# Weighted sums of gathered expert rows: one token's slots per gather and a matmul in place of one slot per gather and a vector add

## The chip, the cores and the metric

The kernel runs on one core of one Trainium2 chip. The metric is the device time of one execution in microseconds (us), lower is better. The core's five engines run side by side, each with its own in-order queue: PE (TensorE, matmuls; PEld is its weight load), DVE (VectorE), ACT (ScalarE), POOL (GpSimd) and SP (SyncE, which here only starts DMAs).

## The reference, cut to what matters

One decoder layer runs for 512 prompt tokens and 32 sample tokens (8 sequences of 4): RMSNorm, an input projection, RWKV-7 time mixing beside windowed attention, an output projection, and then the PEER expert retrieval, which is where the change sits. Each token has 8 heads of 16 chosen experts, so 128 slots; each slot names one of 16,384 rows of `expert_u` and of `expert_v` (1,024 f32 numbers, 4 KB a row).

```python
idx  = ...                                  # (token, 128) expert numbers
gate = softmax(top)                         # (token, 128)
pre  = einsum('td,tkd->tk', hb, eu[idx])    # a dot product per slot
act  = gelu(pre) * gate
out  = einsum('tk,tkd->td', act, ev[idx])   # a scaled sum of 128 rows per token
x    = x + out
y    = rmsnorm(x, final_norm_g)
```

## The kernel before, in words

The prompt is cut into four tiles of 128 tokens. Tiles 1 and 2 (256 tokens) take the expert layer densely: all 16,384 experts in 128 blocks, on PE. Tiles 0 and 3 and the 32 samples gather only the rows that they need. `experts` (L1024) does that: an indirect DMA per step, issued by POOL (L1032), brings 128 rows, one into each partition; 128 steps for `expert_u` (DVE multiplies the buffer by the token's `h2` and sums, `dot`, L1041), then Gelu, then 128 steps for `expert_v` (DVE adds the scaled buffer to `acc`, `add`, L1050). In step k partition p holds the row for slot k of token p. The samples use the 128 partitions as 4 head pairs of 32 tokens, so they take 32 + 32 steps, and at the end `sample_experts` (L1066) brings the four parts together with three small DMAs and four DVE additions. Gathered rows lie in one rotation of five buffers, `gat`; the use of a buffer is written two steps behind its gather (`LAG`, L33).

The program has three stretches. The front (to about 1107 us) holds the projections, the time mixing, attention and the choice of experts (`two_heads`, L970: top-16 searches on DVE). Then `gates` (L1380) spreads the gate values of tiles 1 and 2 into dense tables. Then the dense stage runs its 128 blocks, with tile 3's own front work (`late`, L1507) in its first blocks, and tile 3's gathers beside it.

The gather steps are Python generators in the list `side`; `beside` (L245) takes steps from it. A scheduler then orders the instructions of each engine at build time: what was written earlier has priority, what was written later fills the gaps. `first_gathers` (L1319) puts tile 0's 256 steps into `side`, `sample_heads` appends the samples' 64. No step is written during the front. 280 are written in one go after it (`AHEAD`, L36 and L1552), the other 40 a few at a time between the groups of `gates` (`RATE_G`, L1402) and the first dense blocks (`RATE_D`, L1585); each step's DVE instructions are tied behind a given earlier DVE instruction.

PSUM has eight banks of 128 x 512 f32. In the front six belong to pool `pp` (L1281) as three pairs, `pB` (time mixing), `pC` (attention and the rest) and `pD` (projections), and two to pool `pe` (L232): `pA` (`rwkv_prep`, L282) and `pQ` (`mix_and_retrieve`, L905), one bank each. `fr.close()` (L1361) gives them all back. The dense pool `dp` (L1407) takes all eight: four banks `w`, four `acc`.

Of the kernel before, what the change touches and what calls it, by code (L numbers as in the profile page):

```python
# [32 lines left out]
LAG = 2  # L33
WST = 3
UV = 5
AHEAD = 280  # L36
RATE_G = 0.8
RATE_D = 3.0
LATE = 2
# [74 lines left out]
def hymba_step(ctx, tc, x_prompt, x_sample, cache_k, cache_v, state_wkv, state_shift, meta, norm1_g, w_in, mu, w0,  # L114
# [40 lines left out]
    def gat(shape=(128, D)):  # L155
        return _t(p0, "gat", GAT, shape)

    def px2():
        return _t(p0, "x2", 1, [128, D])
# [19 lines left out]
    def transpose(out, in_):  # L179
# [3 lines left out]
        else:  # L183
            T.matmul(out, in_, ident[:k, :k], start=True, stop=True)


    few = p0.tile([128, 4], F32, name="few")
    epsn, epsg, half3, one = (few[:, i:i + 1] for i in range(4))
# [40 lines left out]
        DM.dma_start(t, const[:, _OFF[c][0]:_OFF[c][0] + 16])  # L229

    er = fr.enter_context(tc.tile_pool(name="er", bufs=1, side="right"))
    pe = fr.enter_context(tc.tile_pool(name="pe", bufs=1, space=PSUM, side="right"))  # L232

    def st(tag, bufs, shape, dt=F32):
        return _t(er if tag in _EARLY else sb, tag, bufs, shape, dt)
# [15 lines left out]
                side.pop(0)  # L251
        due[0] = min(due[0], 1.0)

    def pA():
        return _t(pe, "pA", 1, [128, 512])

    def pB():
        return _t(pp, "pB", 2, [128, 512])

    def pC():  # L260
        return _t(pp, "pC", 2, [128, 512])

    def pD():
        return _t(pp, "pD", 2, [128, 512])

    def pQ():
        return _t(pe, "pQ", 1, [128, 512])

    def h_transposed(h, rows, put, ps):
        for half in range(2):  # L270
# [11 lines left out]
    def rwkv_prep(c0, n, more=None):  # L282
        special, meta_ = n == 40, n == 16
        e = n + 1
        room = [dx([128, D]) for _ in range(3)] if meta_ else None
        pP = pQ if meta_ else pA
        m = (st("mm", 1, [128, 14, 16]) if meta_ else st("m14", 1, [128, 14, 128]))[:, :, 0:n]
        for k0, k1 in ((12, 14), (0, 12)) if more else ((0, 14),):
            DM.dma_start(m[:, k0:k1], mscr[k0:k1, :, c0:c0 + n].rearrange("k p c -> p k c"))
# [10 lines left out]
            gT = m[:, 13, :]  # L300
            A.activation(gT, gT, AF.Sigmoid)
        pw = pP().rearrange("p (a b) -> p a b", a=4)
        pz = (more or pP)().rearrange("p (a b) -> p a b", a=4)
        for b in range(4):
            T.matmul(pw[:, b, 0:n], lora[0:64, b * 128:(b + 1) * 128], th, start=True, stop=True)
            T.matmul(pz[:, b, 0:n], lora[64:128, b * 128:(b + 1) * 128], m[64:128, 12, :], start=True, stop=True)
# [598 lines left out]
    def mix_and_retrieve(items):  # L905
# [37 lines left out]
        for g in range(4):  # L943
            scs = [st(f"sco{x}", 2 - x, [128, 4, 128])[:it[1]] for x, it in enumerate(items[::-1])][::-1]
            for j in range(4):
                if j % 2 == 0:
                    ps = pQ().rearrange("p (i j n) -> p i j n", i=2, j=2)
                hc = 4 * g + j
                wt = weights(w_query, hc)
                p = pD()  # L950
                for k in range(8):
                    T.matmul(p[:, 0:tot], wt[:, k, :], h2T[:, k, :], start=(k == 0), stop=(k == 7))
                qT = st("qq", 2, [128, 160])[:, 0:tot]
                A.copy(qT, p[:, 0:tot])
                for x, (it, o) in enumerate(zip(items, offs)):
                    T.matmul(ps[:it[1], x, j % 2, :], qT[:, o:o + it[1]], skT[:, hc % 2, :], start=True, stop=True)
                if j % 2:
                    for x, (it, sc) in enumerate(zip(items, scs)):
                        A.copy(sc[:, j - 1:j + 1, :], ps[:it[1], x])
            for it, sc in zip(items, scs):  # L960
                if isinstance(it[5], bass.AP):
                    DM.dma_start(it[5][:, 4 * g:4 * g + 4, :], sc)
                else:
                    two_heads(sc, [x[:, 32 * g:32 * g + 32] for x in it[5]], front_tile)
# [56 lines left out]
        V.tensor_tensor(gate, gate, bc(rd.unsqueeze(2), [128, 2, 16]), OP.mult)  # L1021


    def experts(h2, ei, gate, nk, acc, fresh):  # L1024

        pre = _t(p0, "pre", 1, [128, 128])

        def rows(w, use):
            held = []
            for k in range(nk):  # L1030
                r = gat()
                G.indirect_dma_start(out=r, out_offset=None, in_=w[0],  # L1032
                                     in_offset=bass.IndirectOffsetOnAxis(ap=ei[:, k:k + 1], axis=0))
                held.append((k, r))
                if len(held) > LAG:
                    use(*held.pop(0))
                yield True
            for x in held:
                use(*x)

        def dot(k, u):  # L1041
            V.tensor_tensor_reduce(out=u, in0=u, in1=h2, scale=1.0, scalar=0.0, op0=OP.mult, op1=OP.add,
                                   accum_out=pre[:, k:k + 1])
        yield from rows(eu, dot)
        act = _t(p0, "act", 1, [128, 128])
        A.activation(act[:, 0:nk], pre[:, 0:nk], AF.Gelu)
        V.tensor_tensor(act[:, 0:nk], act[:, 0:nk], gate[:, 0:nk], OP.mult)
        acc = acc()

        def add(k, v):  # L1050
            if k == 0 and fresh:
                V.tensor_scalar(acc, v, act[:, 0:1], None, OP.mult)
            else:
                V.scalar_tensor_tensor(acc, v, act[:, k:k + 1], acc, OP.mult, OP.add)
        yield from rows(ev, add)

    def finish(x2, y, rows, dst, gf, kind="F"):

        rms(x2[:rows], y[:rows], rows, gf, kind)
        DM.dma_start(dst, y[:rows])  # L1060

    def final_g(t):
        G.dma_start(t, fin_g.partition_broadcast(128))
        return t

    def sample_experts():  # L1066

        h2S = ph2()
        for kg in range(4):
            G.dma_start(h2S[32 * kg:32 * kg + 32, :], hscr_s)  # L1070
        box = []

        def mk():
            box.append(px2())
            return box[0]
        yield from experts(h2S, plS[0], plS[1], 32, mk, True)
        xs2 = ph2()
        G.dma_start(xs2[0:32, :], xscr_s)
        for kg in range(4):
            part = box[0]  # L1080
            if kg:
                part = gat()
                G.dma_start(part[0:32, :], box[0][32 * kg:32 * kg + 32, :])
            V.tensor_tensor(xs2[0:32, :], xs2[0:32, :], part[0:32, :], OP.add)
        finish(xs2, gat(), 32, y_s.rearrange("b s d -> (b s) d"), final_g(gat()))

    def tile_experts(i, ei, ga, h2, x2=None):
        def mk():
            if x2 is None:
                box.append(px2())  # L1090
                G.dma_start(box[0], xscr[i])
            return box[0]
        box = [] if x2 is None else [x2]
        yield from experts(h2, ei, ga, 128, mk, False)
        finish(box[0], gat(), 128, y_p[0, 128 * i:128 * i + 128, :], final_g(gat()))


    def load_qk(c0, n):
# [9 lines left out]
                   t[:, j, :].rearrange("p (b f) -> p b f", f=5)[:, :, 0:4])  # L1108
        return qk

    def place(c):
        return _t(p0, "ei" + c, 1, [128, 128], I32), _t(p0, "ga" + c, 1, [128, 128])

    plS, pl0, pl1 = place("s"), place("0"), place("1")
    dsel = [[_t(p0, f"dsel{i}{c}", 1, [128, 128]) for c in range(3)] for i in range(2)]
    ycats, zs = {}, {}

# [199 lines left out]
    gather_mark = []  # L1317

    def first_gathers():  # L1319
        side.append(tile_experts(0, *pl0, *held))  # L1320
        gather_mark.append(len(marks))

    def sample_heads():
# [56 lines left out]
    def gates(its, sel, ps, put):  # L1380
# [6 lines left out]
        for n, t8 in enumerate(range(0, 128, 8)):  # L1387
# [12 lines left out]
                put(t8 + q0, p)  # L1400
            with tc.issue_after(marks[-1]):
                beside(RATE_G)  # L1402


    ND = 256
# [101 lines left out]
    def late():  # L1507
# [28 lines left out]
        for g in range(4):  # L1536
# [10 lines left out]
                    A.copy(sc[:, j0 + j, :], p[:, 128:256])  # L1547
                yield True
            two_heads(sc, [x[:, 32 * g:32 * g + 32] for x in pl1], late_tile)
        side.append(tile_experts(3, *pl1, x2))  # L1550

    for n in range(AHEAD):  # L1552
        with tc.issue_after(marks[gather_mark[0]]):
            beside(1)
    more = late()
    its = one_hot_table()
    sels = [sel_transposed(0, dps, dt_("selT", 1, [128, 3, 128])), sel_transposed(1, dps, dt_("lsc", 1, [128, 3, 128]))]
# [73 lines left out]
```

## Time and profile before

| | us |
|---|---|
| median of 3 runs | 2249.78 (2248.66 to 2256.09) |
| the profiled execution, its own time | 2252.27 |
| its span, first to last instruction | 2250.5 |
| PE / DVE / ACT / POOL busy | 1852.8 / 1721.2 / 864.3 / 1499.9 |
| mean granted TensorE clock | 0.869 |

The span is what the trace shows; the execution's own time has 1.8 us around it. A busy time is the sum over the whole span, so it hides that different engines set the pace in different stretches. The granted clock is a share of 2.4 GHz; at any moment it is 1.0 or 0.5, and a number between is a mean over a stretch.

### The profile page before, as it was taken

The page shows a single profiled execution, that of the slowest core. Times are in us where ns is not written, and L with a number is a line of the kernel's source. Part 1 is how long each engine was busy: PE and PEld are TensorE (multiplying, and loading weights), DVE is VectorE, ACT ScalarE, POOL GpSimd, SP SyncE. Part 2 cuts the span into 40 slices and gives each one's busy share as a digit, 9 for nine tenths or more (in the row PEclk, how much of TensorE's full clock was granted, in tenths as well). Part 3 has the DMA queues.
Part 4 walks back from the last instruction along what each step waited for, and adds up shares of the span by engine and source line. Part 5 has one row for each costly group of instructions (what it writes and reads, how often), then busy time and mean ns, then how long its engine had stood idle before and what let it go on. Part 6 is the DMA issues. An engine that isn't in the chain of part 4 may idle for free.

```text
span 2250.5 us, 37333 instructions
## 1 busy us (share of the span) xinstructions
PE 1852.8 (82%) x13915; PEld 1718.7 (76%) x13915; DVE 1721.2 (76%) x3221; ACT 864.3 (38%) x1803; POOL 1499.9 (67%) x1135
## 2 busy tenths in 40 slices
PE   5899975586759769878256887899999999999995
PEld 5889874474637657867255887899999999999995
DVE  5543446888778878899799579987666788879897
ACT  6644422212223314232277534343444444343333
POOL 0110114878764876457577656899888999999996
PEclk9999996555756668989588999999999999999998
DMA  7532472777785898978476777799889998998886
GB/s 225 153 100 75 131 201 89 254 255 235 257 278 171 267 311 275 304 253 288 142 215 219 265 272 260 265 327 330 330 328 328 331 319 315 313 316 309 307 301 208
DMA packets 310155, 569.51 MB, mean 253 GB/s; under 512 B 32787, under 2 KB 194565, under 8 KB 309830
## 3 DMA queue, kind: packets, MB, share of 16 engines
q0 software_dynamic: 84048, 305.70, 39.6%
q1 hardware_dynamic: 225926, 261.43, 35.8%
q8 instruction: 109, 1.79, 0.3%
q14 instruction: 72, 0.59, 0.1%
HBM read 543.07 MB, written 24.60 MB: 252 GB/s over the span
## 4 chain that ended last, share of the span: by engine, by line
PE 37%; DVE 22%; issue 14%; POOL 13%; DMA 11%; ACT 2%; SPq 0%; DVEq 0%; POOLq 0%; ACTq 0%
POOL gat L1032 7%; DVE gat L126 4%; DVE x L126 4%; PE acc L1477 3%; PE pD L218 3%; PE acc L1478 3%; DVE uL L126 3%; PE acc L1476 3%; PE w L1461 3%; PE w L1458 3%; PE w L1459 3%; DMA gat<-in_expert_u_dram,ei 2%; PE w L1444 2%; DMA gat<-in_expert_v_dram,ei 2%; POOL aL L1469 2%
## 5 line engine op out<-in xcount | busy, mean ns | idle before, releaser
L126 DVE SCALAR_TENSOR_TENSOR x<-gat,act,x 128x1024 f32<-128x1024 f32 x287 | 495.3, 1726 | 34.1 <-DMA gat<-in_expert_v_dram,ei 31.9
L1032 POOL DMA_INDIRECT gat<-in_expert_u_dram,ei x256 | 353.7, 1382 | 114.6 <-DVE pre L126 51.7
L1032 POOL DMA_INDIRECT gat<-in_expert_v_dram,ei x256 | 335.8, 1312 | 127.9 <-issue 32.7
L1451 POOL TENSOR_TENSOR vL<-uv,vH 128x1024 fp32r<-128x1024 f32 x128 | 314.7, 2459 | 14.0 <-ACT vH L1450 12.0
L1477 PE MATMUL acc<-aL,vH 128*128 128x256 f32 x1024 | 295.5, 290 | 21.8 <-POOL aL L1469 21.5
L1476 PE MATMUL acc<-aH,vH 128*128 128x256 f32 x1024 | 295.0, 295 | 3.4 <-ACT aH L1468 3.4
L1478 PE MATMUL acc<-aH,vL 128*128 128x256 f32 x1024 | 291.4, 286 | 0.0
L1458 PE MATMUL w<-dhH,uH 128*128 128x256 f32 x1024 | 254.2, 285 | 3.7 <-ACT lsc L1547 1.7
L1459 PE MATMUL w<-dhL,uH 128*128 128x256 f32 x1024 | 252.9, 284 | 0.0
L126 DVE CUSTOM_DVE_ANT_0 gat<-gat,h 128x1024 f32<-128x1024 f32 x160 | 215.6, 1357 | 48.8 <-DMA gat<-in_expert_u_dram,ei 45.0
L1450 ACT CAST vH<-uv 128x1024 fp32r<-128x1024 f32 x128 | 134.5, 1051 | 228.5 <-issue 105.4
L1477 PEld LDWEIGHTS acc<-aL,vH 128*128 128x128 f32 x1024 | 199.2, 195 | 27.9 <-POOL aL L1469 27.8
L126 DVE CUSTOM_DVE_ANT_0 gat<-gat,lx 128x1024 f32<-128x1024 f32 x128 | 204.7, 1623 | 9.0 <-DMA gat<-in_expert_u_dram,ei 9.0
L1458 PEld LDWEIGHTS w<-dhH,uH 128*128 128x128 f32 x1024 | 197.7, 193 | 4.8 <-ACT lsc L1547 2.1
L1478 PEld LDWEIGHTS acc<-aH,vL 128*128 128x128 f32 x1024 | 199.3, 195 | 0.0
L1476 PEld LDWEIGHTS acc<-aH,vH 128*128 128x128 f32 x1024 | 195.2, 194 | 3.9 <-ACT aH L1468 3.9
L1459 PEld LDWEIGHTS w<-dhL,uH 128*128 128x128 f32 x1024 | 197.7, 193 | 0.1
L126 DVE TENSOR_TENSOR uL<-w,uH 128x512 fp32r<-128x512 f32 x256 | 167.4, 682 | 16.4 <-ACT uH L1446 14.1
L1469 POOL TENSOR_TENSOR aL<-ac,aH 128x256 fp32r<-128x256 f32 x128 | 141.3, 1104 | 33.6 <-ACT aH L1468 31.3
L1461 PE MATMUL w<-dhH,uL 128*128 128x256 f32 x1024 | 153.5, 289 | 11.4 <-DVE uL L126 11.1
L126 DVE TENSOR_TENSOR ac<-w,gl 128x128 f32<-128x128 f32 x128 | 49.7, 389 | 139.2 <-ACT w L1463 116.5
L1446 ACT CAST uH<-w 128x512 fp32r<-128x512 f32 x256 | 139.3, 591 | 27.3 <-PE w L1444 16.8
(575 smaller groups left out, 4264.7 us busy)
## 6 DMA issues: line engine op xcount, KB each, us to landing
uv<-in_expert_u_dram SPq DMA_DIRECT2D x128, 512.0 KB
uv<-in_expert_v_dram SPq DMA_DIRECT2D x128, 512.0 KB
wst<-in_w_query_dram SPq DMA_DIRECT2D x48, 512.0 KB
wst<-in_w_out_dram SPq DMA_DIRECT2D x24, 512.0 KB
wst<-in_w_in_dram SPq DMA_DIRECT2D x20, 512.0 KB
h2T<-in_w_in_dram SPq DMA_DIRECT2D x20, 512.0 KB
gscr<-uv SPq DMA_DIRECT2D x10, 1024.0 KB
gl<-gscr SPq DMA_DIRECT2D x16, 512.0 KB
```

Of the source, the lines that this page charges most:

```text
L126: r = getattr(nc.vector, name)(*args, **kw)
L1032: G.indirect_dma_start(out=r, out_offset=None, in_=w[0], in_offset=bass.IndirectOffsetOnAxis(ap=ei[:, k:k + 1], axis=0))
L1446: A.copy(uH[:, ks, :], p)
L1450: A.copy(vH, vn)
L1451: G.tensor_tensor(vL, vn, vH.bitcast(F32), OP.subtract)
L1458: T.matmul(pre, uH[:, k, :], hH[:, k, :], start=(k == 0), stop=False)
L1459: T.matmul(pre, uH[:, k, :], hL[:, k, :], start=False, stop=False)
L1461: T.matmul(pre, uL[:, k, :], hH[:, k, :], start=False, stop=(k == 7))
L1469: return (vH, vL, aH, aL), G.tensor_tensor(aL, ac, aH.bitcast(F32), OP.subtract).ins
L1476: T.matmul(o, vH[:, ds_], aH, start=(j == 0 and d % 2 == 0), stop=False, skip_group_check=True)
L1477: T.matmul(o, vH[:, ds_], aL, start=False, stop=False, skip_group_check=True)
L1478: T.matmul(o, vL[:, ds_], aH, start=False, stop=(j == 127), skip_group_check=True)
```

## The change

For tile 0 and the samples (not for tile 3) the `expert_v` half of `experts` is done another way. The table of expert numbers is turned by PE (a transpose through PSUM, then a copy to `eO`), so that one gather now fetches the 128 slots of *one token*, a slot per partition. The activations are turned in the same way (`at`). ACT makes a 128 x 32 matrix `z`, zero but for one column, which holds the token's 128 activations; PE multiplies: `z` stationary, the 128 x 1,024 buffer moving in two halves of 512, and adds the result to two PSUM banks (`v0`, `v1`), where the token's row is 32q + t. Gathers are used in pairs, of two different q, with four matmuls a pair. 128 gathers stay 128, and 32 stay 32. Two DVE additions from PSUM end a tile; the samples' three part DMAs and four additions go.

The two banks are a pool `vp`; the six others become one rotation `w` for all that `pA`, `pB`, `pC`, `pD` and `pQ` served. `vp` is closed before `dp` opens, so all 320 steps are written ahead of `gates`, and `AHEAD` is gone. The helper tiles `ef` and `at` take the one buffer of `pre`.

```diff
-AHEAD = 280
+    unit = p0.tile([128, 63], F32, name="unit")
+    V.memset(unit, 0.0)
+    V.memset(unit[:, 31:32], 1.0)
-    pe = fr.enter_context(tc.tile_pool(name="pe", bufs=1, space=PSUM, side="right"))
+    vs = ctx.enter_context(ExitStack())
+    vp = vs.enter_context(tc.tile_pool(name="vp", bufs=1, space=PSUM, side="right"))
-    def pA(): return _t(pe, "pA", 1, [128, 512])
-    def pB(): return _t(pp, "pB", 2, [128, 512])
...
+    def bank():
+        return _t(pp, "w", 6, [128, 512])
+    pB = pC = pD = bank
-        pP = pQ if meta_ else pA
+        pP = more or bank
...
+    def summed(ei, nk, per, out):
+        def add(act):
+            n = 4 * per
+            et = _t(p0, "eO", 1, [128, 128], I32)
+            order = [per * (i % 4) + i // 4 for i in range(n)]
+            def turned(src):
+                p = _t(vp, "v0", 1, [128, 512])
+                if nk == 128:
+                    T.transpose(p[:, 0:128], src, ident)
+                else:
+                    for g in range(4):
+                        gs = slice(32 * g, 32 * g + 32)
+                        T.matmul(p[gs, 0:32], src[gs, 0:32], ident[gs, gs], start=True, stop=True)
+                return p[:, 0:n]
+            ef = _t(p0, "pre", 1, [128, 128])
+            V.tensor_copy(ef[:, 0:nk], ei[:, 0:nk])
+            A.copy(et[:, 0:n].rearrange("p (r q) -> p r q", q=4), turned(ef).rearrange("p (q r) -> p r q", q=4))
+            p = turned(act)
+            at = _t(p0, "pre", 1, [128, 128])
+            A.copy(at[:, 0:n], p)
+            va = [_t(vp, f"v{x}", 1, [128, 512]) for x in range(2)]
+            pair = []
+            def use(k, r):
+                q, t = k % 4, k // 4
+                z = _t(p0, "z", 4, [128, 32])
+                A.mul(z, unit[:, 31 - t:63 - t], at[:, order[k]:order[k] + 1])
+                pair.append((q, t, z, r))
+                if len(pair) == 2:
+                    for x in range(2):
+                        for q, t, z, r in pair:
+                            T.matmul(va[x][32 * q:32 * q + 32, :], z, r[:, 512 * x:512 * x + 512], start=(t == 0),
+                                     stop=(t == per - 1))
+                    pair.clear()
+            yield from rows(ev, et, n, use)
+            out(va)
+        return add
+    def plus(x, va):
+        for h in range(2):
+            V.tensor_tensor(x[:, 512 * h:512 * h + 512], x[:, 512 * h:512 * h + 512], va[h], OP.add)
...
+    while side:
+        with tc.issue_after(marks[gather_mark[0]]):
+            beside(1)
+    vs.close()
     ND = 256
     dn = ctx.enter_context(tc.tile_pool(name="dn", bufs=1))
-    for n in range(AHEAD):
-        with tc.issue_after(marks[gather_mark[0]]):
-            beside(1)
```

## Rows read from the trace of the kernel before

**Rows 1.** Busy us of the five engines by stretch, clock, DMA share, GB/s.
```profile
670.00:900.00 230.00, 189.48 (x1089) 156.09 (x1088) 182.97 (x253) 77.42 (x189) 153.79 (x125) 0.71 0.78 254
900.00:1110.00 210.00, 143.39 (x1094) 129.78 (x1094) 194.19 (x713) 50.55 (x146) 123.21 (x140) 0.86 0.80 257
1110.00:1252.00 142.00, 87.64 (x519) 80.45 (x520) 134.42 (x125) 105.33 (x164) 103.61 (x66) 0.81 0.62 197
1252.00:1400.00 148.00, 128.17 (x979) 123.62 (x979) 108.73 (x310) 59.62 (x129) 86.58 (x79) 0.95 0.80 280
```

**Rows 2.** The same, instructions on `act` alone: busy us of DVE and ACT.
```profile
900.00:1110.00 210.00, 44.95 (x34) 0.00 (x0) 0.86 0.80 257
1110.00:1252.00 142.00, 24.24 (x15) 0.23 (x1) 0.81 0.62 197
1252.00:1400.00 148.00, 28.55 (x19) 0.00 (x0) 0.95 0.80 280
```

**Rows 3.** Chain that ended last, shares by line: 900:1110, 1110:1252 and 1252:1400.
```profile
by line: DVE x L126 13.8%; DVE gat L126 12.0%; DVE idxu L126 8.4%; DMA wst<-in_w_query_dram 7.0%; issue 7.0%; DVE hl L126 6.4%; DVE dsel L126 5.9%; DVE vals L126 5.6%; DVE sel L126 4.9%; DVE ce L126 4.5%; DVE sco L126 3.8%; DMA gat<-in_expe
...
by line: DVE uL L126 33.0%; issue 22.9%; DVE vH L126 8.5%; PE w L1399 8.1%; DVE gat L126 7.6%; DVE x L126 6.8%; POOL vH L1394 4.0%; ACT uH L1392 2.8%; DMA uv<-hscr 2.7%; PE w L1424 2.6%; PE w L1368 0.9%; POOL gat L1032 0.7%; ACT lsc L1369 0
...
by line: DMA xscr<-lx 9.9%; PE w L1521 7.0%; DVE lsm L126 6.4%; issue 5.7%; PE w L1543 4.8%; DMA gat<-x 4.8%; DVE x L126 4.7%; DVE lidx L126 4.6%; DVE gat L126 4.5%; PE w L1461 4.2%; PE w L1458 3.9%; PE w L1459 3.7%; DVE uL L126 3.4%; DVE l
```

**Rows 4.** Instructions on `gat`: ns min/median/max, first and last start (first row 670:1010).
```profile
L126 DVE SCALAR_TENSOR_TENSOR x<-gat,act,x x128: 1243/1283/3686, 675.8 to 1003.4; 128x1024 f32<-128x1024 f32 x128
...
L1032 POOL DMA_INDIRECT gat<-in_expert_v_dram,ei x256: 932/1017/2605, 663.8 to 2230.9; - x128
L1032 POOL DMA_INDIRECT gat<-in_expert_u_dram,eis x32: 937/976/2015, 1026.3 to 1150.9; - x32
L1032 POOL DMA_INDIRECT gat<-in_expert_v_dram,eis x32: 933/1188/1873, 1158.5 to 1331.6; - x32
```

**Rows 5.** Groups by shape, 1110:1252, DVE: busy us, mean ns, idle before.
```profile
L126 DVE CUSTOM_DVE_ANT_0 gat<-gat,h 128x1024 f32<-128x1024 f32 x11 | 18.5, 1688 | 0.0
```

**Rows 6.** The chain that ended last, in order of time: waits for gathered rows.
```profile
784.01 9.26 DMA gat<-in_expert_v_dram,ei
...
808.53 6.54 DMA gat<-in_expert_v_dram,ei
```

**Rows 7.** PE timeline, narrow matmuls with 512 moving columns: start, us, merged count.
```profile
484.19 1.97 PE L699 MATMUL pC<-wst,sco 40*64 40x512 f32 x4
485.90 1.97 PE L700 MATMUL pC<-wst,sco 40*64 40x512 f32 x4
...
504.95 1.21 PE L699 MATMUL pC<-wst,sco 40*64 40x512 f32 x4
505.99 1.02 PE L700 MATMUL pC<-wst,sco 40*64 40x512 f32 x4
```

**Rows 8.** ACT: a line on 128 x 32, and Gelu of tile 0.
```profile
L1017 ACT ACTIVATE dsel<-dsel x8: 229/229/233, 919.4 to 1099.9; 128x32 f32<-128x32 f32 x8
...
L1046 ACT ACTIVATE act<-pre x1: 309/309/309, 675.1 to 675.1; 128x128 f32<-128x128 f32 x1
```

**Rows 9.** Timeline where the front ends: its last instruction, the next DMA.
```profile
1106.36 0.69 DVE L126 TENSOR_REDUCE dsel<-ce 128x32 f32<-128x512 f32 x1 [1.44 <-POOL ce L1011]
1107.11 0.82 SPq L1419 DMA_DIRECT2D uv<-hscr  x2
```

**Rows 10.** By tile: who writes and reads `hscr`, `ps`, `pQ`; first and last start.
```profile
L936 SPq DMA_DIRECT2D hscr<-dx x2: 319/326/332, 878.1 to 1011.5; - x2
...
L223 ACT COPY po<-ps x4: 359/368/372, 86.8 to 101.9; 128x255 f32<-128x255 f32 x4
...
L305 PE MATMUL pQ<-mm,lora x8: 259/259/280, 90.6 to 91.4; 64*128 64x16 f32 x8
```

**Rows 11.** By line and tile: PE's queue ahead of `gates`, and the first `acc`.
```profile
L1424 PEldq EVENT_SEMAPHORE  x2: 51/16334/32618, 1078.4 to 1111.1; - x2
...
L1476 PE MATMUL acc<-aH,vH x1024: 274/283/562, 1265.5 to 2231.3; 128*128 128x256 f32 x171
```

## What was predicted before the change ran

> **What bounds the kernel now.** I read the busy time by stretch first [rows 1]. Where the front ends, DVE is full: 194 of 210 us in 900:1110 and 134 of 142 in 1110:1252, the stretch of `gates`. PE is not: 143 of 210 and 88 of 142. The chain that ended last agrees [rows 3]: in 900:1110 its first entries are DVE's, with the adds to be removed ("DVE x") the largest at 13.8%, and in 1110:1252 DVE again leads. The instructions on `act` alone [rows 2] show how much of DVE is these adds: 45 us in 900:1110, 24 in 1110:1252, 29 in 1252:1400. So on the face of it the change takes work from the engine that is the bound.
>
> Then I looked at what starts `gates`, because the change writes all steps ahead of it. The reader is to see one thing in the timeline [rows 9]: the front's last instruction, a DVE reduction, ends at 1107.05, and at 1107.11 the next stretch's first load leaves. That load reads `hscr`, whose last part left at 1011.5 [rows 10], 96 us earlier. It did not wait for data. It waited until the pool of the front had been given back *whole*. PE's queue shows it from the other side [rows 11]: it stood for 32.6 us, from 1078.4 to 1111.1, for the first matmul of `gates`. PSUM shows the like: the banks `ps` of the projections were in use to 102.3, while `pQ`, in a pool of its own, could be written from 90.6 [rows 10].
>
> **The change, part by part.**
>
> *The adds leave DVE.* Their time on the chain is 13.8% of 210 = 29.0 us, 6.8% of 142 = 9.7 and 4.7% of 148 = 7.0 [rows 3]. What is late next behind them is the point of the rest.
>
> *The adds on PE.* A pair of gathers takes four matmuls of 32 columns by 512. The nearest row is the narrow f32 product with 512 columns: eight passes, in two column groups side by side, took 505.99 + 1.02 - 504.95 = 2.06 us in one burst and 3.68 in another [rows 7], as the clock stood at one or the other level. 64 pairs of tile 0 are 132 to 236 us of PE, 16 pairs of the samples 33 to 59. PE is busy 189 + 143 = 333 of 440 us in 670:1110, at granted clocks of 0.71 and 0.86 [rows 1]; that work would be 189.5 x 0.71 + 143.4 x 0.86 = 258 us at full clock. 258 + 132 = 390 fits into 440, if the added work brings the clock up. I take the fit, and put its failure among the rivals.
>
> Entering narrow products costs something: the first four passes of the burst took 1.21 us, the next four 1.02 [rows 7], so 0.19 us a switch and, in and out, 0.38 a pair. The Trainium skill, "TensorEngine Tiling", section Key Properties, says that a change of tiling mode drains TensorE; by that rule these 0.38 us are lost on each of 64 pairs, an estimate of 24 us of PE, where the sum above has none. The row is one burst beside other work, so it doesn't settle it.
>
> *ACT* gets 160 `z` of about 0.23 us [rows 8], 37 us, hidden as long as ACT is busy 128 of 440 [rows 1]. In front of each stands a wait for one of four `z` buffers; what is queued behind it on ACT are evacuations for the front.
>
> *The turn from `expert_u` to `expert_v`.* Now the first `expert_v` gather leaves at 663.8 [rows 4], 11 us before Gelu at 675.1 [rows 8]. After the change it needs the turned table, which shares the buffer of `pre`, so it can leave after Gelu only, at about 678. A gather that the chain waited for took 6.5 to 9.3 us more [rows 6], so the first use is at about 686, not 675.8: +10 for tile 0. The samples have the same turn; there I count 14 us from the last dot product to the first product.
>
> *The pace.* Tile 0's uses ran from 675.8 to 1003.4 [rows 4], 327.6 / 127 = 2.58 us each. A pair holds its buffers longer: half a pace (1.3 us) for the partner and 0.7 more for the use, 2.0 / 5 buffers = 0.4 a step at most, 51 us over the tile; at least nothing, or a gain where DVE held the buffers. I take 10 us, near the low end, since five buffers alone don't set this pace. So tile 0 ends at 1003 + 10 + 10 = 1023, and the samples start about where they did (1026.3 [rows 4]): their products need the buffer of `pre`, free when the last `z` is made.
>
> *The samples, now ahead of `gates`.* Before, their steps ran to 1331.6 [rows 4] beside `gates` and the first blocks. Now their pool must be given back before any bank of `dp` is written. 32 + 32 steps at a pace between 1.74 us (issue 0.93 + flight 6.54 + use 1.24, over five buffers) and 4.0 (their own on a full DVE, 124.6 / 31 [rows 4]); I take 2.2, nearer the low end, because the front's DVE work ends on the way. 1026 + 70 + 14 + 70 + 3 for the two additions = 1183. That is when PE may begin `gates`, against 1111.1: **+72** (bounds 1154 and 1230 or more: +43 and +120).
>
> *`gates` without the samples.* It ran from 1111.1 to the first `acc` at 1265.5 [rows 11]. What leaves DVE there is 18.5 us of dot products [rows 5] and 24.2 of adds [rows 2]; on the chain they are 7.6% + 6.8% of 142 = 20 us. ACT's 105 of 142 is the next limit. I take **-35** (between -20 and -43).
>
> *The first dense blocks* lose the last adds (7.0 us on the chain) and the bringing together of the four parts (DMA gat<-x, 4.8% of 148 = 7.1): **-14** (between 0 and -36).
>
> *One rotation of six banks.* Neither `pA` nor `pQ` is among the entries of the chain in 900:1110, so I count no gain; the loss is that the preparation of the 16 meta tokens, on `pQ` at 90.6, must now wait for `ps` to be given back, 12 us, beside projections that fill PE there. Zero.
>
> The sum: 72 - 35 - 14 = +23. The profiled execution took 2252.3 us, so 2275; it lies 2.5 above the median of the runs, so **2272**. The front's own gain on DVE (29 us) isn't in it: the front ends sooner, and then waits for the samples.
>
> **Rivals.**
>
> *The gathers run faster.* Without adds on a full DVE the buffers come free sooner. At 2.2 us tile 0 ends at about 970; the samples' table, 29 us earlier, then is last, at 997, and at 2.0 us a step they end at 997 + 128 + 17 = 1142: +31 - 35 - 14 = -18, 2232. It decides where the samples end before 1160. For it: DMA moves 254 to 257 GB/s in 670:1110 and 280 in 1252:1400 [rows 1]; against: a pair waits for two. 0.20.
>
> *The banks come back one by one*, so that only two of `dp` wait. Then `gates` starts with the front's end: -29 - 10 - 7 - 7 = -53, +10 for PE's share, 2207. Against it stand [rows 9 to 11]. 0.08.
>
> *PE becomes the bound.* Where the granted clock in 670:1110 stays at 0.85, PE needs 258 / 0.85 + 64 x 2.55 = 467 of 440: +27, and the samples, at 2.6 us, end at 1053 + 166 + 17 = 1236: +125 - 35 - 14 = +76, about 2325. It decides below a clock of 0.9 (287 + 152 = 439); the switches' 24 us move that point up. For it: 333 of 440 busy. Against: the clock was 0.95 where PE was busy 128 of 148 [rows 1]. 0.20.
>
> *Gains and losses meet*, within 0.3% (6.7 us, about what a measurement of this kernel tells from no change): 2250. 0.10.
>
> **The numbers.** Forecast 0.42 with a range of its own of 2257 to 2295; the rivals as above. Faster: 0.20 + 0.08 = 0.28; same: 0.10, and 0.01 of the forecast; slower: 0.41 + 0.20 = 0.61. The range leaves out the far ends of the first bank case and of the PE case: 2205 to 2330.
>
> **What would show it.** In the profile after: no matmul on the banks of `dp` before the last addition from `v0`/`v1`; PE's queue standing at L1424's counterpart for about 100 us after the front's last matmul; that addition at 1154 to 1230; DVE's work in the front down by the 45 us of 900:1110 at least [rows 2]; a granted clock above 0.9 in 670:1110; about 119 us from `gates`' first matmul to the first `acc`. Wrong it is if `gates` starts with the front's end, if the samples end before 1160, or if the front's scheduling with six shared banks shifts by tens of us, which I can't bound.

## The result, and the profile after

The changed kernel takes 2606.31 us (median of 4 runs, 2596.68 to 2608.19) against 2249.22 us before: a ratio of 1.159, 95% interval 1.155 to 1.163. That is slower, as forecast in sign, but far outside the range of 2205 to 2330.

The first fence has busy times by stretch of the kernel after, columns as in [rows 1].

```profile
100.00:250.00 150.00, 115.45 (x738) 94.85 (x738) 29.72 (x78) 47.81 (x124) 10.52 (x19) 0.62 0.08 22
...
1375.00:1505.00 130.00, 97.42 (x501) 84.84 (x500) 28.94 (x61) 33.19 (x88) 11.86 (x12) 0.59 0.03 8
...
1508.00:1633.00 125.00, 90.41 (x609) 82.54 (x609) 107.96 (x97) 111.50 (x183) 84.11 (x47) 0.90 0.47 151
1633.00:1780.00 147.00, 135.73 (x1075) 131.50 (x1073) 102.17 (x350) 59.15 (x119) 78.55 (x74) 0.99 0.72 247
```

The last two rows answer to `gates` and the first blocks of [rows 1]: DVE falls from 134 of 142 us to 108 of 125 in `gates`, as expected. The first two have no place in the forecast. The kernel before does this in 100:250 (same view):

```profile
100.00:250.00 150.00, 145.07 (x1169) 125.10 (x1169) 56.68 (x110) 69.89 (x164) 10.71 (x20) 0.94 0.30 87
```

It gets 1169 matmuls through where the kernel after gets 738, and moves 87 GB/s where the kernel after moves 22. And in 1375:1505 of the kernel after nothing but the samples' last normalisation (to 1381) is left of tile 0 and the samples, DMA moves 8 GB/s, and PE works at a clock of 0.59 for 130 us more. What it works on there is the time mixing and the attention of tile 3, the strands that are written last (a strand here is a chain of work, such as the projections, a tile's time mixing or its attention, whose steps wait for each other). Two views of the same kernel date these: instructions on `gat` (ns min/median/max, first and last start) answer to [rows 4],

```profile
L221 PEld LDWEIGHTS w<-gat,wst x360: 186/190/334, 272.6 to 391.0; 128*128 128x128 f32 x180
L1035 POOL DMA_INDIRECT gat<-in_expert_v_dram,eO x160: 932/946/1460, 844.9 to 1364.4; - x160
L1035 POOL DMA_INDIRECT gat<-in_expert_u_dram,eis x32: 939/946/1977, 1188.4 to 1259.5; - x32
```

and the timeline where the front ends answers to [rows 9, 11].

```profile
1499.31 0.58 ACT L1391 COPY dx<-w 128x512 f32<-128x512 f32 x1
1500.18 0.57 SPq L1393 DMA_DIRECT2D yscr<-dx  x1
1504.04 0.80 SPq L1463 DMA_DIRECT2D uv<-hscr  x2
...
1507.83 2.58 PE L1468 MATMUL w<-ident,uv 128*128 128x128 f32 x11 [8.78 <-DMA uv<-hscr]
...
1632.73 0.47 PE L1520 MATMUL acc<-aH,vH 128*128 128x256 f32 x1
```

The first `expert_v` gather leaves at 844.9 and not 663.8; the samples, meant to bind the start of `gates`, made their last gather at 1364.4. `gates` waits until 1507.8 for the front itself. So in the spans of the two profiles: the first matmul of `gates` 1111.1 to 1507.8, **+396.7**; `gates` 154.4 to 124.9, **-29.5**; from the first `acc` to the end 985.0 to 972.4, **-12.6**; sum 354.6 = 2605.1 - 2250.5. The last two terms were forecast at -35 and -14. All that is missing lies in the front.

### The profile page after: what moved, and what is told of

Read it like the earlier page. It is cut to its first block, busy times and chain, and to the rows that moved or that the text cites. A ratio compares the mean times of both kernels' runs of the same rounds, so it can differ in the third digit from the quotient of the medians.

```text
span 2605.1 us, 38865 instructions
## 1 busy us (share of the span) xinstructions
PE 2104.0 (81%) x14573; PEld 1797.6 (69%) x14573; DVE 1552.6 (60%) x3065; ACT 922.1 (35%) x1973; POOL 1424.4 (55%) x1136
## 4 chain that ended last, share of the span: by engine, by line
PE 38%; issue 15%; POOL 15%; DVE 12%; DMA 10%; ACT 4%; DVEq 0%; POOLq 0%; SPq 0%; ACTq 0%
POOL gat L1035 8%; PE v L1079 5%; PE w L945 3%; POOL vL L1495 3%; DMA h2T<-in_w_in_dram 3%; POOL aL L1513 3%; DVE uL L125 2%; PE acc L1521 2%; PE w L181 2%; DVE gat L125 2%; PE acc L1522 2%; PE acc L1520 2%; PE w L485 2%; PE w L490 2%; PE w L1505 2%
## 5 line engine op out<-in xcount | busy, mean ns | idle before, releaser
L1035 POOL DMA_INDIRECT gat<-in_expert_u_dram,ei x256 | 343.2, 1341 | 89.6 <-issue 42.6
L125 DVE SCALAR_TENSOR_TENSOR x<-gat,act,x 128x1024 f32<-128x1024 f32 x128 | 283.3, 2214 | 13.7 <-DMA gat<-in_expert_v_dram,ei 12.5
L1035 POOL DMA_INDIRECT gat<-in_expert_v_dram,eO x160 | 156.0, 975 | 202.3 <-PE v L1079 157.0
L1079 PE MATMUL v<-gat,z 128*32 128x512 f32 x640 | 224.1, 621 | 15.7 <-DMA gat<-in_expert_v_dram,eO 13.5
L125 DVE CUSTOM_DVE_ANT_0 gat<-gat,h 128x1024 f32<-128x1024 f32 x160 | 203.1, 1282 | 50.6 <-DMA gat<-in_expert_u_dram,ei 35.0
L125 DVE CUSTOM_DVE_ANT_0 gat<-gat,lx 128x1024 f32<-128x1024 f32 x128 | 229.1, 1811 | 5.1 <-DMA gat<-in_expert_u_dram,ei 5.1
L1035 POOL DMA_INDIRECT gat<-in_expert_v_dram,ei x128 | 185.6, 1450 | 24.2 <-issue 16.9
```

The costliest lines, as they stand in the source:

```text
L125: r = getattr(nc.vector, name)(*args, **kw)
L1035: G.indirect_dma_start(out=r, out_offset=None, in_=w[0], in_offset=bass.IndirectOffsetOnAxis(ap=ei[:, k:k + 1], axis=0))
L1079: T.matmul(va[x][32 * q:32 * q + 32, :], z, r[:, 512 * x:512 * x + 512], start=(t == 0), stop=(t == per - 1))
```

## The experiments

**Which part of the change does it.** The change has two that reach the front: the sums on PE and the PSUM rotation. Theory A blamed the second, theory B the first. e1 is the kernel before with the rotation alone; e2 is e1 with 8 in place of the 6.

```diff
-    def pA():
-        return _t(pe, "pA", 1, [128, 512])
...
+    def bank():
+        return _t(pp, "w", 6, [128, 512])
+    pB = pC = pD = bank
-        pP = pQ if meta_ else pA
+        pP = more or bank
```

> The kernel before with one part of the change: all PSUM users of the front draw from one rotation of six banks; the adds of expert_v stay on DVE and the samples stay beside gates. Theory A (a rotation hands its banks out in the order in which the code was written, so strands that had groups of their own now run one behind the other): the front ends 300 to 400 us late, near 1400 to 1500 us of the span, the first projection matmul on a gat buffer is near 270 us instead of 117, and the whole takes 2550 to 2650 us. Theory B (the adds on PE, with the waits of PE and ACT in front of them, make the front late): about 2250 us, the front ending at 1107 us.

> As the first kernel, with eight banks in the one rotation, as many as the groups before had together. Theory A1 (it is the shared order that costs): nearly as slow as with six, 2500 to 2650 us, the first projection matmul on a gat buffer still past 230 us. Theory A2 (it is the two banks that are missing): back to 2250 us within 1%.

Measured: e1 2607.08 us, 1.158 (1.151 to 1.165); e2 2613.72, 1.160 (1.153 to 1.167). The rotation alone, with every add still on DVE, costs all that the whole change costs; and eight banks cost as much as six. It is the sharing, not the number. The first projection matmul on a `gat` buffer starts at 279.7 us in e1 and 280.5 in e2 (117.5 before), as theories A and A1 said. Theory B falls as the explanation of the 357 us. That the two totals agree so closely is partly chance: e1's front is 360.6 us longer than before and the whole change's 396.7, so the rest of the change costs 36 us there and gives 38 back behind it.

What the sharing does is seen in the matmuls of one line. L218 (L221 after) is the projections, written as `project_rest()` behind `attend(0)`, `meta_wkv()` and `local(0)` (the line also has the first projections, on `ps`, which end at 102 us before and at 128 in e1); the stretches show PE's busy time on that line alone (PE, PEld, clock, DMA share, GB/s). Kernel before:

```profile
100.00:190.00 90.00, 39.88 (x230) 33.42 (x229) 0.92 0.32 90
190.00:280.00 90.00, 45.46 (x265) 39.04 (x265) 0.98 0.37 109
```

e1, the same line, and below it its L485, the inverse within the time mixing (here of the meta tokens and of tile 0):

```profile
190.00:280.00 90.00, 0.30 (x2) 0.32 (x3) 0.60 0.00 1
280.00:400.00 120.00, 87.39 (x480) 78.50 (x478) 0.91 0.39 116
```

```profile
190.00:280.00 90.00, 18.20 (x128) 17.48 (x128) 0.60 0.00 1
280.00:400.00 120.00, 0.00 (x0) 0.00 (x0) 0.91 0.39 116
```

Before, the projections run through 100:280, beside the time mixing (its counterpart, L497, has 131 matmuls there). In e1 they have two matmuls in 190:280, beside the time mixing's 128; when its strand is through, they come in one piece. These rows cover the first 121 us of the loss (the first `expert_u` gather leaves at 456.2 against 335.4 before). The rest builds up later in the front: the inverse's last matmul starts at 964.1 before and at 1406.1 in e1.

**Is it the written order?** e5 is e1 with one line moved.

```diff
+    project_rest()
     attend(0)
     meta_wkv()
     local(0)
     wkv_chain(*locals_[0], ycat(0))
-    project_rest()
```

> The first kernel (one rotation of six, adds on DVE) with one line moved: project_rest() stands ahead of attend(0), meta_wkv() and local(0) in the code, not behind them; the banks and their sharing stay as they are. Theory A (banks are handed out in the order of the code): the first projection matmul on a gat buffer goes from 272 to about 115 us, the first gather of expert_u and the end of the front come 100 to 160 us earlier, 2440 to 2510 us in all. If the sharing costs whatever the order (too few banks at a time, or waits of the engines): 2580 us or more.

Measured: 2626.54 us, 1.173 (1.168 to 1.177). The time was expected to fall and didn't; it is that of the case named against theory A (2580 us or more). But the order turned round as theory A says, with the first projection matmul on a `gat` buffer at 139.0 us: L218 and then L485 in e5,

```profile
100.00:190.00 90.00, 57.48 (x342) 52.65 (x343) 0.85 0.29 83
190.00:280.00 90.00, 52.72 (x284) 46.94 (x283) 0.85 0.36 107
280.00:400.00 120.00, 0.00 (x0) 0.00 (x0) 0.51 0.00 1
```

```profile
190.00:280.00 90.00, 0.00 (x0) 0.00 (x0) 0.85 0.36 107
280.00:400.00 120.00, 19.87 (x128) 19.15 (x128) 0.51 0.00 1
```

The projections are first now, and the time mixing follows in 280:400 with DMA idle. Whoever comes first, one strand runs behind the other, so the sum stays: the first `expert_u` gather at 475.8 us against 456.2 in e1. Too few banks, the other reading of this time, is ruled out by e2 (eight banks, and as slow) and by e6 below (eight banks, and 173 us faster than e1). So the reading that fits all of these runs is: a slot of a rotation goes to its users in the order in which they are written, and what is written later gets no slot before what stands ahead of it has had its own, even where their engines could work side by side. What e5's expectation had wrong was the price of the order, not the order.

**Who must not share.** e6 gives the projections (and the scores of `mix_and_retrieve`, once on `pQ`) a pair of their own beside the rotation of six, eight banks as in e2.

```diff
-    pB = pC = pD = bank
+    pB = pC = bank
+    def pD():
+        return _t(pp, "pD", 2, [128, 512])
```

> The first kernel with a pair of banks of its own for the projections (pD) beside the rotation of six, eight in all, as the second kernel has, which shared all eight. Theory A: the projections no longer stand in the order of the others, the first one on a gat buffer is near 115 to 140 us, and 150 us or more of the 360 come back: 2300 to 2460 us. If it doesn't matter who shares with whom: 2600 us.

Measured: 2434.59 us, 1.085 (1.082 to 1.088): 173 of the 359 us come back, with as many banks as e2, and the first projection matmul on a `gat` buffer starts at 136.2. Time mixing, attention and the early preparations still share, and this front ends near 1293 us.

**The change without its rotation.** e3 is the whole change, e4 the kernel before, each with six banks as three pairs.

```diff
-    def bank():
-        return _t(pp, "w", 6, [128, 512])
-    pB = pC = pD = bank
+    def pB():
+        return _t(pp, "pB", 2, [128, 512])
...
-        pP = more or bank
+        pP = more or (pC if meta_ else pB)
```

> The whole change, but its six banks in three groups of two (one for attention and the token tiles' preparation, one for the meta tokens' preparation and the recurrence, one for the projections) in place of one rotation; the sums stay on PE. Theory A: the front ends within 100 us of where it did before (1107 to 1200 us), the samples then bind the start of gates as forecast, and the whole takes 2210 to 2330 us. Theory B: 2500 us or more, since the sums are still on PE.

> The kernel before with its front in the same three groups of two banks, the adds on DVE, the samples beside gates: what six banks cost without the shared order. Theory A: 2240 to 2290 us, since the preparations only share with one other strand each. If the number of banks is what costs: 2400 us or more.

Measured: e3 2394.23 us, 1.064 (1.060 to 1.069); e4 2314.99, 1.030 (1.026 to 1.035). e3 wins back 212 us with the sums still on PE, but both are above their ranges, so two more costs were open: +67 for the pairs alone, and +79 for the sums on top.

**Why three pairs still cost.** PE's waits in 30:130 of e4, the largest first (us, times, longest):

```profile
PE ps L331 <- POOL pa L329: 16.2, 1, 16.2
```

The same written order, in the first 130 us: the preparation of tile 0 (`more`) now takes *both* its banks from the projections' rotation `ps`, and the projections written behind it stand while POOL works for it. `ps` is last read at 128 us instead of 102, and the meta tokens wait for it. e9 (from e4) and e10 (from e3) give the two early preparations two banks of their own again, `pA` and `pQ`; in e9 they are in a pool `pe` as before, in e10 they are `v0` and `v1`, idle at that time.

```diff
-        pP = more or (pC if meta_ else pB)
+        pP = pQ if meta_ else pA if more else pB
-        pz = pP().rearrange("p (a b) -> p a b", a=4)
+        pz = (more or pP)().rearrange("p (a b) -> p a b", a=4)
```

> The fourth kernel (three pairs, adds on DVE) with the two banks that the groups pA and pQ had given to the two early preparations alone, those of the first token tile and of the meta tokens; everything later stays in the pairs. Theory E (the whole price of the three pairs is early: the preparation of the first tile takes slots in the order of the projections' own rotation, which stand behind it for 26 us, and the meta tokens wait for that rotation to be given back): the projections' last bank is read at 102 us again and not at 128, gates start near 1111 instead of 1176, 2245 to 2270 us. If the pairs cost later in the front: above 2290 us.

> The third kernel (the whole change with three pairs) with the same two early preparations in the banks v0 and v1, which stand idle until tile 0's sums. Theory E: 55 to 65 us come back as with the sums on DVE, 2325 to 2345 us; what is left over the kernel before is then the sums on PE with the samples ahead of gates, +75 to +95. If the early loss is hidden behind the sums on PE: 2370 us or more.

Measured: e9 2269.36 us, 1.011 (1.005 to 1.016); e10 2351.58, 1.047 (1.042 to 1.053). Of the 67 us of e4 46 come back, and 43 of e3's: theory E is right for most of it (`ps` read last at 102.4 again), but not for all: e9 lies at the top of its range and e10 above its own (2325 to 2345), since some 20 us of pairs lie later in the front (`gates` starts at 1127.5 in e9, not 1111). e10 is thus the change as it was forecast, with only these 20 us left of what the merged groups cost: +105 instead of +23.

**What the sums on PE cost.** Busy times of e10 by stretch (PE, PEld, DVE, ACT, POOL, clock, DMA share, GB/s), cut at tile 0's first `expert_v` gather (716), its last sum (1131) and the first matmul of `gates` (1253), and then the sums alone in the second stretch:

```profile
670.00:716.00 46.00, 37.18 (x146) 30.55 (x146) 35.45 (x70) 10.95 (x24) 24.03 (x21) 0.50 0.68 240
716.00:1131.00 415.00, 404.83 (x2523) 258.68 (x2521) 177.02 (x765) 147.94 (x430) 199.72 (x245) 0.97 0.75 239
1131.00:1253.00 122.00, 51.68 (x147) 12.45 (x148) 43.08 (x71) 17.23 (x47) 72.98 (x68) 0.71 0.85 299
1253.00:1379.00 126.00, 87.50 (x608) 78.54 (x606) 109.16 (x98) 113.39 (x191) 84.09 (x47) 0.92 0.44 140
```

```profile
716.00:1131.00 415.00, 161.24 (x513) 32.41 (x513) 1.08 (x2) 0.27 (x1) 0.97 0.75 239
```

PE is full: 405 of 415 us at a clock of 0.97, 161 of them the sums, while DVE has dropped to 177. In order of time (start, us, line), sums and the front's own products take turns on PE:

```profile
818.65 1.90 PE L1090 MATMUL v<-gat,z 128*32 128x512 f32 x4
...
820.98 1.06 PE L922 MATMUL pD<-wst,dx 128*128 128x128 f32 x8
821.97 1.94 PE L922 MATMUL pD<-wst,yTs 128*32 128x128 f32 x16
...
856.72 1.02 PE L1090 MATMUL v<-gat,z 128*32 128x512 f32 x2
```

From 828 to 856 only the front's own products run, most of them the output projection's (L922), without a gap, and the gathers stop behind the sums that wait for PE: POOL waits 135.5 us for them in this stretch.

```profile
POOL gat L1046 <- PE v L1090: 135.5, 60, 13.7
```

So tile 0 ends at 1131 and not at 1023. e7 tests it: e3 with half of the products left out (the upper 512 columns are not summed).

```diff
-                    for x in range(2):
+                    for x in range(1):
                         for q, t, z, r in pair:
```

> The third kernel (the sums on PE, three pairs of banks) with half of the products left out: the upper 512 columns of the sums are not computed (the lower ones are added in their place). All gathers, z and waits stay. Theory C (with the sums PE is the bound in tile 0's expert_v phase: it was busy 398 of 401 us at a clock of 0.99 there, 155 of them the sums): tile 0's steps go from 3.08 to 2.5 to 2.7 us, the start of gates comes 50 to 70 us earlier, 2325 to 2345 us. Theory D (the pairs hold the gathers' buffers, or ACT's z come late): the pace stays near 3 us and the time within 15 us of 2394.

Measured: 2346.57 us, 1.045 (1.042 to 1.049), 48 below e3; `gates` starts 52 us earlier and a step of tile 0 takes 2.77 us instead of 3.08. Theory C holds in the main, though the pace stops a little short of what it expected (2.5 to 2.7): in e7 too PE is busy 352 of the 361 us from the first `expert_v` gather of tile 0 to its last sum.

**The samples ahead of `gates`.** e12 is e10 with the samples' steps beside `gates` again, their sums in the banks of `acc2` and `acc3` (`vbox` names where sums go).

```diff
-    while side:
+    while len(side) > 1:
         with tc.issue_after(marks[gather_mark[0]]):
             beside(1)
     vs.close()
...
+    vbox.append([(dp, "acc2"), (dp, "acc3")])
+    for n in range(24):
+        with tc.issue_after(marks[gather_mark[0]]):
+            beside(1)
...
     gates(its, sels[1], dps, keep)
+    while side:
+        with tc.issue_after(marks[gather_mark[0]]):
+            beside(1)
+    acc += [_t(dp, f"acc{c}", 1, [128, 2, ND]) for c in (2, 3)]
```

> The tenth kernel with one more thing undone: only tile 0's sums stand ahead of gates, the samples' steps run beside gates as before, their sums on PE in the banks of acc2 and acc3. Theory F (the samples ahead of gates, about 130 us of steps with PE nearly idle, cost about 100 us, and taking them out of gates gives 26 back): gates start at the end of tile 0's sums, near 1115 to 1130, take about 155 us, and the whole 2255 to 2290 us. If PE is so full with tile 0's sums that the front itself ends 100 us later: 2320 us or more.

Measured: 2330.38 us, 1.037 (1.032 to 1.042): 21 us less than e10. The time is that of the case against theory F (2320 or more), but not its reason: `gates` did start at 1132.0, as theory F said, 121 us earlier than in e10; but then it took 183.7 us instead of 126.2, and the dense part 1006 instead of 970.5. The samples' 64 steps cost about 93 us beside `gates` and the blocks, and 121 ahead of them. All the samples come after the front here; before, 26 of their gathers left beside it.

**Is there anything to win in `gates`?** e8 is the kernel before with the samples' sums alone on PE (in `acc2`, `acc3`, so nothing is ahead of `gates`); e11 is e8 with half of the products left out, as e7; e13 leaves the samples' `expert_v` steps out of the kernel before, with zeros in their place. In the diff, the core of e8, of e11 and of e13 (`fresh` is set for the samples alone):

```diff
-        yield from experts(h2S, plS[0], plS[1], 32, mk, True)
+        yield from experts(h2S, plS[0], plS[1], 32, None, False, summed(plS[0], 32, 8, out))
...
-                    for x in range(2):
+                    for x in range(1):
...
         acc = acc()
+        if fresh:
+            V.memset(acc, 0.0)
+            return
```

> The kernel before (its five groups of banks, tile 0's adds on DVE, the samples beside gates) with the samples' sums alone on PE, in the banks of acc2 and acc3, which nothing else uses until the blocks begin. DVE loses 53 us of adds between the end of the front and the first blocks, and nothing is put ahead of gates. If these adds are what the change could win: the first acc 5 to 25 us earlier and the first blocks 13 us shorter, 2205 to 2235 us. If the samples' end then binds the blocks (acc2 and acc3 are wanted back at 1265 us): 2245 to 2270 us.

> The eighth kernel (only the samples' sums on PE, beside gates) with half of the products left out: the upper 512 columns are not summed. Theory C (the adds freed DVE, but the products fill PE, which was busy 110 of 117 us in 1175:1292 at a clock of 0.99): the first acc comes 15 to 25 us earlier, 2220 to 2235 us. If the gathers or the order of the steps set the end of the samples: within 8 us of 2247.

> The kernel before with the samples' expert_v steps (32 gathers and 32 adds) left out, zeros in their place; the dot products stay. Theory G (the gathers on POOL and the adds on DVE together hold gates): gates go from 154 to 130 to 135 us and the first blocks shorten by 13, 2205 to 2225 us. If it is the dot products that hold gates: 150 us and more, 2235 to 2250 us.

Measured: e8 2247.38 us, 0.998 (0.994 to 1.001); e11 2250.64, 1.002 (0.999 to 1.006); e13 2230.91, 0.994 (0.991 to 0.996). So e8 lands in the second case of its expectation, e11 too, and e13 between its two ranges. e13 sets the ceiling for the samples' half of the change: with their `expert_v` steps gone altogether, gathers and adds, the kernel gains 16 us. In its profile `gates` takes 145.4 us (154.4 before), the dense part 970.8 (985.0). The fence shows 1110:1258 and 1258:1400 of e13, columns as above,

```profile
1110.00:1258.00 148.00, 96.00 (x605) 88.62 (x606) 126.90 (x125) 115.76 (x193) 95.26 (x58) 0.81 0.50 161
1258.00:1400.00 142.00, 131.22 (x1039) 127.38 (x1037) 98.17 (x341) 58.53 (x118) 73.72 (x71) 0.98 0.73 252
```

and this one the same stretches of e8, with its samples' products by tile below.

```profile
1110.00:1258.00 148.00, 118.08 (x672) 85.28 (x671) 114.31 (x116) 118.81 (x210) 114.76 (x86) 0.88 0.70 232
1258.00:1400.00 142.00, 138.38 (x1035) 123.99 (x1033) 83.91 (x320) 56.45 (x120) 64.68 (x68) 1.00 0.71 249
```

```profile
L1076 PE MATMUL acc<-gat,z x128: 589/592/617, 1179.6 to 1291.6; 128*32 128x512 f32 x128
```

In e8 DVE has less to do than in e13, and PE 22 us and POOL 20 us more; `gates` takes 158.7 us. The samples end at 1292 in e8, 1293 in e11: past the first `acc`, halved products or not, so theory C has no hold there; the gathers or the written order of the steps are left.

e14 puts every second product of `gates` on DVE (e8 with `GV = 2` for 3), e15 writes the samples' steps closer as well (`RATE_G = 1.4` for 0.8), e16 is the kernel before with `GV = 2`.

```diff
-RATE_G = 0.8
+RATE_G = 1.4
...
-GV = 3
+GV = 2
```

> The eighth kernel (only the samples' sums on PE, beside gates) with every second product of gates on DVE in place of every third (GV 2), the rest on POOL. Theory G (the samples' gathers on POOL, 38 x 1.1 us in gates, hold POOL's products, and DVE has room since the adds are gone): gates go from 159 to 145 to 152 us, 2230 to 2242 us. If neither POOL nor DVE is the limit there: within 6 us of 2247.

> The same with the samples' steps written at 1.4 to each step of gates in place of 0.8. If the samples' end (1292 us in the eighth kernel, past the first acc) holds the first blocks, which want acc2 and acc3 back: it comes 20 to 30 us earlier and the whole 5 to 12 us below the kernel with GV 2 alone, 2220 to 2235 us. If more gathers in gates only push POOL's products back: the same or slower, 2240 to 2260 us.

> The control: the kernel before with GV 2, the adds on DVE. DVE is busy 139 of 158 us in gates, and 11 more products are 20 us of work or more: slower by 0 to 15 us, 2250 to 2265 us, under any theory in which DVE is full there.

Measured: 2248.11 us, 1.001 (0.998 to 1.004); 2248.04, 1.000 (0.997 to 1.002); 2246.39, 1.000 (0.997 to 1.003). None can be told from the kernel before, and none of the gains and losses that were expected came. e16 tells most: with DVE full in `gates`, as the prediction read it, every second product on DVE was to cost up to 15 us, and more than 7 are outside its interval. In e14's profile `gates` falls to 150.6 us, but the dense part, 987.6, gives it back (978.7 in e8); the samples still end at 1292 there. In e15 they end at 1286, 6 us earlier for the 20 to 30 expected, so the order in which they are written has little hold on it. These spans are of one profile each, and the times of the kernel before alone spread from 2231 to 2260 us, so differences of some us between them are not shown. No version that does the whole work beats the kernel before.

## Why the prediction was wrong, point by point

- **One rotation of six banks: "Zero". This is the step that failed.** It asked which banks stood on the chain in 900:1110, found none, and counted one 12 us wait; the loss begins long before, with 112 us by the first `expert_u` gather (447.9 against 335.4). The groups were not a bound; they were what let strands written one behind the other run at the same time. The rotation alone costs 359 us (e1) and the number of banks nothing (e2); 173 come back when the projections get a pair of their own (e6), 292 with three pairs (e4), 338 when the early preparations get theirs too (e9). The last clause of the prediction, a shift of the front "which I can't bound", was the one that came true; it should have been a rival with a price. [Rows 10] had the evidence: `pQ` written at 90.6 while `ps` was in use to 102.3.
- **The forecast's own frame, the samples ahead of `gates`**, was right where the rotation is gone. In e10 the first matmul of `gates` follows the last addition from `v0` and `v1` by 0.1 us: +141.5, against +72. In the kernel as changed the frame never came to bear, since the front ended last. The turn was +14 (723.8 against 709.9 in e9) for +10; the samples took 122 us for 160.
- **The pace, +10 over tile 0, was mis-sized**: it was 406 / 127 = 3.2 us a step in e10, 2.56 in e9, so about +80. The work was nearly right: 258 + 132 = 390 us of PE at full clock were forecast from 670 on, and e10 has 37.2 x 0.50 + 404.8 x 0.97 = 411 in 670:1131. The slip was to fit it into 440 us counted from 670: the sums' first gather leaves at 716, and until then PE runs at 0.50.
- **The rival "PE becomes the bound"** (2325, chance 0.20) is what e10 shows, at 2352, or some 2330 without the 20 us of pairs, but not by its condition: it needed a clock below 0.9, and the clock was 0.97. In 716:1131 PE is full at nearly the full clock. That the times lie so near is luck: the rival had tile 0 end at 1053 and the samples take 183 us, and in e10 it was 1131 and 122.
- **The switch of 0.38 us a pair** (0.19 in and out): the sums took 160.9 us of PE for 64 pairs (the 161.24 of the row has the turn of the tables in it), 2.51 each, where the forecast's 2.06 is 2.12 at a clock of 0.97, so 25 us more. That is the size of the 24 us estimated by the Trainium skill's rule ("TensorEngine Tiling", Key Properties: a change of tiling mode drains TensorE). The trace agrees with the size. e3 and e7, the same but for half of the products, say a little more; their sums alone over tile 0, e3 and then e7:

```profile
768.00:1172.00 404.00, 154.83 (x512) 30.32 (x512) 0.99 0.76 243
```

```profile
765.00:1126.00 361.00, 95.82 (x256) 12.66 (x256) 0.96 0.84 273
```

  Half of the products take 62% of the time. At full clock a pair is 154.8 x 0.99 / 64 = 2.40 us with four products and 95.8 x 0.96 / 64 = 1.44 with two, so 0.48 a pair, 31 us over the tile, doesn't go with the number of products: an estimate from these two rows. No run here takes the switches away, so that they are this part is not shown.
- **`gates` without the samples, -35**: -29.5 in the kernel after, -28 in e10. The size was right, the reason half right. The adds and gathers of `expert_v` are worth 9 us of it (e13, one profile); the remaining 20, by difference, would belong to the dot products and their gathers, which was not tried alone.
- **The first dense blocks, -14**: -12.6 after, -14.5 in e10, -14.2 in e13. The size came out, the split did not: e13 leaves out the steps alone and still brings the four parts together, so the 7.1 counted for that are not borne out.
- **"The adds leave DVE"**: 29 us of chain in 900:1110 were counted as given back to the front. They were not: where DVE fell to 177 of 415 us, PE rose to 405. What tile 0's adds really cost the front before is open, since no run leaves them out.

## What to carry to other kernels

A rotation of buffers is also an order: its slots go out as the code is written, so merging the groups of independent strands puts one behind the other, with the same number of buffers or more. Before pooling buffers, list which strands run at the same time in the trace, and keep a group for each; a group that never shows in the chain of waits may be what keeps a wait from arising. And when work moves from a full engine to one that looks half idle, count the taker's work in the stretch in which the new work can really start, at the clock granted there.

## What was not expected of the hardware

PE busy did not mean a high clock. All of PE's work in two stretches (columns as in [rows 1]), in the kernel before and then in e1:

```profile
100.00:190.00 90.00, 85.07 (x542) 70.11 (x541) 38.72 (x74) 45.85 (x105) 10.71 (x20) 0.92 0.32 90
190.00:280.00 90.00, 89.34 (x854) 82.69 (x853) 34.46 (x71) 38.75 (x87) 8.45 (x10) 0.98 0.37 109
```

```profile
100.00:190.00 90.00, 60.38 (x354) 47.36 (x354) 17.32 (x46) 36.27 (x87) 10.51 (x19) 0.66 0.14 36
190.00:280.00 90.00, 84.77 (x607) 75.29 (x607) 16.43 (x41) 20.57 (x60) 1.27 (x1) 0.60 0.00 1
```

In 190:280 PE counts as busy for 84.8 of 90 us in e1 and got 0.60, after 60.4 of 90 us at 0.66 in 100:190; the kernel before, busy 89.3 of 90 us there after 85.1 of 90, got 0.98. What e1 ran there was the time mixing's dependent chains, nearer to 1.2 GHz than to 2.4, so its work also lasts longer: tile 0's matmuls of the inverse there are 80 in 16.4 us of PE, 0.21 each, against 61 in 8.0, 0.13 each, on L497 of the kernel before. So one strand at a time costs twice: PE has more idle time, and the strand itself runs slower. Busy time times clock is 166 us of work at full clock in 100:280 of the kernel before and 91 in e1. Of the 75 missing, about 28 are the 29 us more in which PE is idle, 25 of them in 100:190, and about 47 are the lower clock; this split is an estimate from the four rows. No run holds the clock, so what e1 would take at the clock of the kernel before is open.
